# Attention steps two half chunks apart, projections in turns in the halves of one PSUM bank, DMA-made blocks in a value chunk's second half, first operands copied

## The chip, the cores and the metric

The kernel runs on one core of one Trainium2 chip. The metric is the device time of one execution in microseconds; a time is the median of several runs. The engines are named as in the profile: PE (TensorE, the matrix engine), DVE (VectorE), ACT (ScalarE), POOL (GpSimd) and SP (SyncE, which issues most transfers).

## The reference

A two-layer encoder on 256 tokens of width 2048, in fp32. Each layer is an attention part and an MLP of hidden width 8192:

```python
for i in range(DEPTH):                                   # 2 layers
    n = rms_norm(h, attn_norm[i])
    if i % N_MIXERS == 0:                                # layer 0: neighbourhood attention
        z = n @ a_w_in[j]
        q, k, v, qm = jnp.split(z, [MIX_WIDTH, 2 * MIX_WIDTH, 3 * MIX_WIDTH], axis=-1)
        mix = neighbourhood_attention(...)               # 12 heads of 128, a bias per head
    else:                                                # layer 1: grouped-query attention
        ...
    km, vm = jnp.split(m @ w_mem_kv[i], 2, axis=-1)
    cross = memory_attention(...)                        # 4 heads, 256 memory tokens
    h = h + jnp.concatenate([mix, cross], axis=-1) @ w_o[i]
    n = rms_norm(h, mlp_norm[i])
    h = h + jnp.square(jax.nn.relu(n @ w_up[i])) @ w_down[i]
return rms_norm(h, final_norm)
```

The change lies in layer 0's attention part: the projections to `qm` (4 memory heads), `q` and `k` (12 mix heads each) and `v` (12 heads), and the heads' scores, softmax and product with the values.

## The kernel before

**Exact products.** Every fp32 operand x is split in two: `hi`, a copy in the matrix engine's format made by ACT (L500), and `lo` = x - hi, made by DVE (L501). A product is three matmuls: hi·hi, lo·hi and hi·lo.

**Chunks.** Weights are read in chunks of 128x2048 fp32 (1024 KB). A chunk is worked in two half chunks, and the half chunk is the clock of the program. `run_all` goes through a list of half chunks; `ahead` runs the stages of later ones: their load eight half chunks ahead, their `pre` five and their `prep` (the splits) three. `later(n, fn)` runs `fn` n half chunks later. What comes out is handed to a scheduler that simulates the engines and may still move instructions; its result is the order that the listings below show.

**Projections (kind S).** One chunk makes one head's q, k or qm, transposed: 48 matmuls of 128x256 into a PSUM tile `ps_s` (L404). DVE reads it out scaled by the norm's row factor (`summed`, L545: qm_s, q_s, k_s); ACT and DVE split the result (qmT, qT, kT). There are 4 + 12 x 2 = 28 such chunks. With a chunk that follows one of another kind, `entered_half` makes the first 128 columns of lo apart from the rest.

**Values.** The values of a group of four heads come from four chunks by a scheme of seven products instead of eight: p1 to p7, each summed over the chunks in half a bank of PSUM (`v_ps`, four banks; tile ps_v, L882). `value_grains` (L838 to L890) gives each value chunk two half chunks ("grains"). Of a chunk's four 512-column blocks b0 to b3, products p1, p2 and p4 use a block as it was loaded or with another added, the others use sums of blocks. `pre` makes these in `v_t`: one copy on ACT (L849), two sums on DVE (L850, L852), and two on DMA, which adds while it moves: POOL issues b3 += b1 in the loaded tile (raw<-raw) and block 2 of v_t += block 1 (v_t<-v_t). The left operands are parts of the normed input, or its sums (`left`, made by `x_d` on DVE, L823, and a split). After the fourth chunk `values_done` combines the seven products (v_c, L903) and splits the result into `va` (L693 on ACT, L694 on DVE).

**Heads.** `attention` runs each head in four steps at set distances in half chunks: `attend` (scores into `sc_ps`, L557 to L559, bias L566, max L568, exp L570, 1/sum L573, scale L578); `turned` (DVE transposes in 32x32 squares, L615, and four SP transfers that put the squares in place, L620, tile pT_t); `halved` (pT_t is split); `attend3` (av, L634 to L636, then the split into `cat`). The distances are in `steps`, counted from `at`: (0, 1, 3, 4), starting one half chunk after the projection.

**Order around the change.** The plan alternates: one projection chunk, then one value half chunk (two of them behind the fifth and sixth projection), until the 24 value half chunks are used up; the last projections follow each other.

**Room.** In layer 0, PSUM has five banks in the pool `acc` and three in `att` (scores and av). `v_ps` holds four of acc's banks while a value group is summed, so that one is left for projections. The pools: ring (tiles `raw`, three; hi and lo, four), `spare` (`sums`: one v_t), work, `cat`, which also has a small unused tile `pad`.

Of the kernel before, what the change touches and what calls it, by code (L numbers as in the profile page):

```python
# [10 lines left out]
F32 = mybir.dt.float32  # L11
F32R = mybir.dt.float32r
BF16 = mybir.dt.bfloat16
AF = mybir.ActivationFunctionType
ALU = mybir.AluOpType
AX = mybir.AxisListType

P = 128
D = 2048
SEQ = 256  # L20
# [4 lines left out]
NH = 12  # L25
NKV = 4
NMH = 4
# [7 lines left out]
HALF = CH // 2  # L35
# [26 lines left out]
LEFT = 16  # L62
# [95 lines left out]

class Grain:

    kind, last_block = "G", False

    def __init__(self, run, after=None, load=None, pre=None, prep=None, ahead=(8, 5, 3)):
        self.run, self.after, self.stages, self.ahead = run, after, (load, pre, prep), ahead
# [3 lines left out]
def encoder_kernel(ctx: ExitStack, tc: tile.TileContext, t: dict, out: bass.AP):  # L168
    nc = tc.nc
# [27 lines left out]
    def open_ring():  # L197
        at.ring = opened("ring")
        at.cat = opened("cat")

        for pool in (at.ring, at.cat):
            pool.tile([P, 64], F32, tag="pad", name="pad")

    def open_work():
        at.work = opened("work", side="right", bufs=2)
# [25 lines left out]
    for q in range(4):  # L231
        s = slice(q * 512, (q + 1) * 512)
# [113 lines left out]
    def new_half(kind):  # L346
        s = slice(STILL_AT // 4, STILL_AT // 4 + HALF) if kind == "S" else slice(0, HALF)
        return tuple(at.ring.tile([P, HALF + n], F32R, tag=x, bufs=4, name=x)[:, s] for x, n in LONGER.items())
# [11 lines left out]
    def later(n, fn, *args):  # L360
        pending.append((state["tick"] + n, fn, args))
# [105 lines left out]
    def add_s(src, acts, done, place=None):  # L467

        def start(w):
            if place != 1:  # L470
                box["ps_s"] = at.acc.tile([P, 512], F32, tag="acc", name="ps_s")
            w.ps = box["ps_s"][:, (place or 0) * SEQ :][:, :SEQ]
        plan.append(Work("S", src, acts, 0, True, True, start, done))
# [24 lines left out]
    def split(dst_hi, dst_lo, src):  # L498

        first = nc.scalar.activation(dst_hi, src, AF.Copy)  # L500
        return first, nc.vector.tensor_tensor(dst_lo, src, dst_hi.bitcast(F32), op=ALU.subtract)  # L501
# [141 lines left out]
    def attention(jobs, at, gap=1, steps=(0, 1, 3, 4), rest=0):  # L643


        def step(n, job, prev):
            qT, kT, bias, v, head, cat = job
            if n == 0:
                res = attend(qT, kT, bias)
            elif n == 1 and len(steps) == 4:  # L650
                res = turned(prev)
            elif n < len(steps) - 1:
                res, box["pT", head] = (halved if len(steps) == 4 else attend2)(prev)
            else:
                if "between" not in box:
                    return attend3(prev, v, head, cat)
                with tc.issue_after(box.pop("between").ins):
                    return attend3(prev, v, head, cat)
            results[n, head] = res

        results = {}
        for t in range(len(jobs) + len(steps) - 1):
            for n in range(len(steps)):
                if 0 <= t - n < len(jobs):
                    j = t - n
                    more = rest if n == len(steps) - 1 and j == len(jobs) - 1 else 0
                    later(at + gap * j + steps[n] + more,
                          lambda n=n, job=jobs[j]: step(n, job, results.get((n - 1, job[4]))))
# [4 lines left out]
    def get(name):  # L673
        return lambda: box[name]
# [8 lines left out]
    def keys(name):  # L683
        return at.work.tile([P, NMH, 512], F32R, tag="keys", bufs=1, name=name)
# [4 lines left out]
    def head_of(v, hd):  # L689
        return lambda part, kt: (box[v] if isinstance(v, tuple) else v)[:, part, kt, hd * HD : (hd + 1) * HD]  # L690
# [59 lines left out]
            add_s(t[f"w_km{layer}"][hd], get("memT"), km_done(layer, hd), 1 if (layer, hd) == (0, 3) else None)  # L750
        add_m([t[f"w_vm{layer}"][c] for c in range(4)], parts_of("memT"), vm_done(layer), layer == 0)

    mem_sq = at.work.tile([P, 512], F32, tag="b_o", bufs=3, name="mem_sq")

    def mem_squares(j):
        m = mem0[:, j * 512 : (j + 1) * 512]
# [73 lines left out]

    GH = 4

    PARTS = (("p3", "p1", "p2", "p5"), ("p7", "p6", "p4"))
    PLACES = {"p3": (0, 0), "p1": (0, 1), "p2": (1, 0), "p5": (1, 1), "p7": (2, 0), "p6": (2, 1), "p4": (3, 0)}
    RAW = {"p1": (0, 1), "p2": (1, 1), "p4": (1, 0)}
    SUM = {"p5": 0, "p7": 1, "p6": 2, "p3": 3}

    def value_grains(g, c, begins, ends):  # L838

        own = {}  # L840

        def load():
            own["b"] = at.ring.tile([P, CH], F32, tag="raw", bufs=3, name="raw")
            nc.sync.dma_start(own["b"], t["w_av"][g * 4 + c])

        def pre():
            b = own["b"].rearrange("p (a b) -> p a b", a=4)
            s = own["t"] = at.spare.tile([P, 3, 512], F32, tag="sums", name="v_t")
            nc.scalar.activation(s[:, 2, :], b[:, 2, :], AF.Copy)  # L849
            nc.vector.tensor_tensor(s[:, 0, :], b[:, 3, :], b[:, 0, :], op=ALU.add)  # L850
            nc.gpsimd.dma_start(b[:, 3, :], b[:, 1, :], accum_op=ALU.add)
            nc.vector.tensor_tensor(s[:, 1, :], s[:, 0, :], b[:, 1, :], op=ALU.add)  # L852
            nc.gpsimd.dma_start(s[:, 2, :], s[:, 1, :], accum_op=ALU.add)

        def prep(n):
            src = own["t"].rearrange("p a b -> p (a b)") if n else own["b"]
            for m in range(2):
                x = src[:, m * HALF : min((m + 1) * HALF, src.shape[-1])]
                hi, lo = (y[:, : x.shape[-1]] for y in new_half("S"))
                split(hi, lo, x)  # L860
                own[n, m] = hi, lo

        def left(name, q, part):
            if name in RAW:
                e, i = RAW[name]
                return box["nT"][:, (2 * c + q) * 2 + e, part * SEQ + i * P :][:, :P]
            return box["left", c][:, q, part, SUM[name], :]

        def run(n):
            if begins and n == 0:  # L870
                box["v_ps"] = [at.acc.tile([P, 512], F32, tag="acc", name="ps_v") for _ in range(4)]
            for m in range(2):
                hi, lo = own.pop((n, m))
                for q in range(2):
                    for a, name in enumerate(PARTS[n][2 * m : 2 * m + 2]):
                        bank, half = PLACES[name]
                        ps = box["v_ps"][bank][:, half * SEQ : (half + 1) * SEQ]
                        s = slice(a * 512 + q * SEQ, a * 512 + (q + 1) * SEQ)
                        begin, end = begins and q == 0, ends and q == 1
                        for part, x, st, sp in ((0, hi, begin and half == 0, False), (0, lo, False, False),  # L880
                                                (1, hi, False, end)):
                            ins = nc.tensor.matmul(ps, left(name, q, part), x[:, s], start=st, stop=sp,  # L882
                                                   skip_group_check=True)
                            if x is hi and part == 0:
                                pin(ins)

        def after():
            if ends:
                values_done(g)

        return [Grain(lambda: run(0), None, load, pre, lambda: prep(0)),
                Grain(lambda: run(1), after, None, None, lambda: prep(1))]

    def values_done(g):

        p = {name: box["v_ps"][bank][:, half * SEQ : (half + 1) * SEQ] for name, (bank, half) in PLACES.items()}
        c = at.work.tile([P, NT, 2, SEQ], F32, tag="pT", name="v_c")
# [19 lines left out]
    def a_k_done(hd):  # L917
        def f(w):
            k = at.work.tile([P, 512], F32R, tag="b_y2", name="kT")
            s = summed(w.ps, "k", box["x_row"])  # L920
            split(k[:, :SEQ], k[:, SEQ:], s)
            b = at.work.tile([P, BJ * GRID_W], F32, tag="b_o", bufs=3, name="bias")
            nc.sync.dma_start(b, t["bias"][hd])
            attention([(box.pop(("q", hd)), k, b, head_of(("v", hd // GH), hd % GH), hd, box["cat"])], 1)
        return f

    def a_qm_done(hd):
        def f(w):
            if hd == 0:
                box["cat"] = at.cat.tile([P, KT, 512], F32R, tag="cat", name="cat0")  # L930
            q = at.work.tile([P, 512], F32R, tag="b_y", name="qmT")
            s = summed(w.ps, "qm", box["x_row"], SCALE)
            split(q[:, :SEQ], q[:, SEQ:], s)
            attention([(q, box["km"][:, hd, :], None, head_of(box["vm"], hd), NH + hd, box["cat"])], 1)
        return f

    CHUNKS = (2, 0, 1, 3)
    with_values = [x for g in range(NH // GH) for n, c in enumerate(CHUNKS) for x in value_grains(g, c, n == 0, n == 3)]
# [1 line left out]
    for hd in range(NH):  # L940
        projections += [(t["w_aq"][hd], a_q_done(hd)), (t["w_ak"][hd], a_k_done(hd))]
    for n, (src, done) in enumerate(projections):
        add_s(src, get("nT"), done)
        for _ in range(1 + (n in (4, 5))):
            if with_values:
                plan.append(with_values.pop(0))
# [833 lines left out]
```

## Time and profile before

| | us |
|---|---|
| median of 3 runs | 2050.93 (2050.22 to 2051.31) |
| profiled execution, its own time | 2049.45 |
| its span | 2047.6 |
| attention part of layer 0 in which PE is not full | about 101 to 380 |

The page gives each engine's busy time, then the span in 40 equal slices of 51.2 us with the busy share in tenths; `PEclk` is the clock granted to PE. The windows view cuts the span at chosen times. The waits view sums what an engine's instructions waited for. A row of a timeline gives start, duration, engine, line, operation, and in brackets the idle time before it with what ended it.

### The profile page before, as it was taken

How to read it: one execution, taken by the hardware profiler on the slowest of the kernel's cores; microseconds unless marked ns; L12 is line 12 of the kernel's file. 1: busy time of each engine (PE TensorE's matmuls, PEld its weight loads, DVE VectorE, ACT ScalarE, POOL GpSimd, SP SyncE). 2: the span in 40 equal slices, each digit the busy share in tenths (PEclk: the TensorE clock that was granted, in tenths of full speed). 3: DMA queues.
4: the chain of work that ended last, by engine and by line, in shares of the span. 5: the costliest groups of instructions: out<-in, count | busy, mean ns of one | idle time of the engine just before them, and what ended most of it. 6: DMA issues, size and time to landing. Idle time of an engine off the chain costs nothing.

```text
span 2047.6 us, 33383 instructions
## 1 busy us (share of the span) xinstructions
PE 2006.2 (98%) x13136; PEld 1826.6 (89%) x13136; DVE 1760.5 (86%) x2126; ACT 1376.8 (67%) x1933; POOL 144.3 (7%) x169
## 2 busy tenths in 40 slices
PE   9977989999999999999999999999999999999998
PEld 8877989989999999999998888889999999999997
DVE  7777788668989999999999778778989999999997
ACT  6755656557777777777776566566777777777774
POOL 0001010000000000000000011000000000000000
PEclk9988999999999999999999999999999999999999
DMA  7856677667777777777765865368777777777772
GB/s 298 290 171 170 206 205 256 205 221 235 230 236 232 226 237 231 227 237 229 236 225 167 290 193 196 129 229 264 232 224 240 226 238 232 221 243 227 228 235 103
DMA packets 109311, 456.46 MB, mean 223 GB/s; under 512 B 11360, under 2 KB 38752, under 8 KB 61536
## 3 DMA queue, kind: packets, MB, share of 16 engines
q1 hardware_dynamic: 88704, 417.08, 58.0%
q0 software_dynamic: 20160, 36.71, 11.0%
q8 instruction: 103, 1.69, 0.3%
q10 hardware_dynamic: 288, 0.52, 0.1%
q14 instruction: 56, 0.46, 0.1%
HBM read 400.27 MB, written 4.19 MB: 198 GB/s over the span
## 4 chain that ended last, share of the span: by engine, by line
PE 92%; DVE 3%; DMA 2%; issue 1%; ACT 1%; SPq 0%; DVEq 0%; POOL 0%; POOLq 0%; ACTq 0%
PE ps_u L404 34%; PE p L1230 9%; PE p L1228 9%; PE p L1231 9%; PE ps_s L404 7%; PE ps_m L381 6%; PE ps_m L385 6%; PE ps_m L384 6%; PE ps_v L882 2%; DVE lo L501 1%; DMA mem_k<-km_w 1%; DMA raw<-in_w_aqm 1%; ACT hi L500 0%; PE av L635 0%; PE av L636 0%
## 5 line engine op out<-in xcount | busy, mean ns | idle before, releaser
L404 PE MATMUL ps_u<-hT,uh 128*128 128x256 f32 x3812 | 663.4, 276 | 0.0
L404 PEld LDWEIGHTS ps_u<-hT,uh 128*128 128x128 f32 x3812 | 578.9, 188 | 5.5
L404 PE MATMUL ps_u<-hT,ul 128*128 128x256 f32 x1960 | 541.4, 276 | 0.0
L500 ACT ACTIVATE uh<-raw_U 128x1024 fp32r<-128x1024 f32 x262 | 277.2, 1060 | 208.4 <-PE ps_u L404 195.6
L404 PEld LDWEIGHTS ps_u<-hT,ul 128*128 128x128 f32 x1960 | 368.0, 188 | 0.0
L501 DVE TENSOR_TENSOR lo<-raw,hi 128x1024 fp32r<-128x1024 f32 (+1 forms) x218 | 258.3, 1192 | 97.7 <-ACT hi L500 96.8
L501 DVE TENSOR_TENSOR ul<-raw_U,uh 128x1024 fp32r<-128x1024 f32 x262 | 319.1, 1222 | 15.5 <-ACT uh L500 15.5
L501 DVE TENSOR_TENSOR tl<-t,th 128x2048 fp32r<-128x2048 f32 x116 | 265.8, 2291 | 71.4 <-ACT th L500 71.0
L500 ACT ACTIVATE hi<-raw 128x1024 fp32r<-128x1024 f32 (+1 forms) x218 | 223.3, 1035 | 150.8 <-PE ps_m L385 74.2
L500 ACT ACTIVATE th<-t 128x2048 fp32r<-128x2048 f32 x116 | 222.9, 1921 | 118.1 <-PE p L1231 114.8
L501 DVE TENSOR_TENSOR bl<-b,bh 128x1536 fp32r<-128x1536 f32 x116 | 203.3, 1753 | 0.0
L1228 PE MATMUL p<-th,a_s 128*128 128x512 f32 x464 | 181.2, 391 | 0.0
L1197 POOL DMA_DIRECT2D t<-b x116 | 100.3, 865 | 1144.4 <-ACT t L1196 1052.6
L1230 PE MATMUL p<-tl,a_s 128*128 128x512 f32 x464 | 181.0, 390 | 0.0
L1231 PE MATMUL p<-th,a_s 128*128 128x512 f32 x464 | 180.5, 389 | 0.0
L500 ACT ACTIVATE bh<-b 128x1536 fp32r<-128x1536 f32 x116 | 172.8, 1490 | 7.7
L404 PE MATMUL ps_s<-nT,hi 128*128 128x256 f32 x896 | 159.9, 279 | 7.5 <-DVE k_s L545 4.6
L404 PEld LDWEIGHTS ps_s<-nT,hi 128*128 128x128 f32 x896 | 136.6, 188 | 9.0 <-ACT hi L500 5.0
L1231 PE MATMUL p<-bh,a_s 128*128 128x512 f32 x348 | 136.2, 391 | 0.0
L1230 PE MATMUL p<-bl,a_s 128*128 128x512 f32 x348 | 135.7, 390 | 0.0
L1228 PE MATMUL p<-bh,a_s 128*128 128x512 f32 x348 | 135.4, 389 | 0.0
L404 PE MATMUL ps_s<-nT,lo 128*128 128x256 f32 x448 | 124.9, 279 | 2.1 <-DVE lo L501 2.1
(328 smaller groups left out, 3788.7 us busy)
## 6 DMA issues: line engine op xcount, KB each, us to landing
raw_U<-in_w_up SPq DMA_DIRECT2D x128, 1024.0 KB, 5.5
b<-in_w_pair SPq DMA_DIRECT2D x116, 1024.0 KB, 5.8
raw<-in_w_o SPq DMA_DIRECT2D x32, 1024.0 KB, 5.0
t<-b POOLq DMA_DIRECT2D x116, 256.0 KB, 5.2
raw<-in_w_b SPq DMA_DIRECT2D x21, 1024.0 KB, 5.1
raw<-in_w_av SPq DMA_DIRECT2D x12, 1024.0 KB, 5.0
raw<-in_w_aq SPq DMA_DIRECT2D x12, 1024.0 KB, 5.4
raw<-in_w_ak SPq DMA_DIRECT2D x12, 1024.0 KB, 5.1
```

The source lines that it names most:

```text
L381: first = nc.tensor.matmul(ps, ah, hi[:, s], start=st, stop=False)
L384: nc.tensor.matmul(ps, ah, lo[:, s], start=False, stop=False)
L385: final = nc.tensor.matmul(ps, al, hi[:, s], start=False, stop=sp)
L404: ins = nc.tensor.matmul(ps, x, acts[:, k, part], start=k == n == 0, stop=k == KT - 1 and n == 2)
L500: first = nc.scalar.activation(dst_hi, src, AF.Copy)
L501: return first, nc.vector.tensor_tensor(dst_lo, src, dst_hi.bitcast(F32), op=ALU.subtract)
L882: ins = nc.tensor.matmul(ps, left(name, q, part), x[:, s], start=st, stop=sp, skip_group_check=True)
L1197: nc.gpsimd.dma_start(s[:, 3, :], b[:, 1, :], accum_op=ALU.add)
L1228: ins = nc.tensor.matmul(ps, a[:, 0, ai, :], hi[:, s], start=begins, stop=False)
L1230: nc.tensor.matmul(ps, a[:, 0, ai, :], lo[:, s], start=False, stop=False)
L1231: nc.tensor.matmul(ps, a[:, 1, ai, :], hi[:, s], start=False, stop=ends)
```

## The change

Six edits, all for layer 0's attention part.

1. A projection that follows a value half chunk now counts as following another kind (`Grain.kind` "M"), so its lo is made in two pieces (128 and 896 columns) and the first matmuls go lo before hi.
2. All 28 projections share one tile `ps_s` of acc, and take its left and right 256 columns in turns.
3. Products p5 and p7 change places: both blocks that DMA finishes (for p4 and p5) are now used in a value chunk's second half. v_t has four blocks instead of three; ACT copies two; the first DMA adds into v_t instead of the loaded tile. `prep` splits five pieces instead of four.
4. The memory heads and mix heads 0 to 7 start two half chunks after their projection and take their steps at (0, 2, 4, 6); heads 8 to 11 keep one and (0, 1, 3, 4).
5. Eight 128x128 left operands, those of the first matmul of each value half chunk, are copied by ACT to a place of their own (`entries`), eight half chunks after the last memory head; from then on those matmuls read the copies.
6. `cat`'s unused tile is gone, and a tile `mem_sq` used at the very start moves from the work pool to `spare`.

```diff
 class Grain:
-    kind, last_block = "G", False
+    kind, last_block = "M", False
...
-        for pool in (at.ring, at.cat):
-            pool.tile([P, 64], F32, tag="pad", name="pad")
+        at.ring.tile([P, 64], F32, tag="pad", name="pad")
...
     def add_s(src, acts, done, place=None):
         def start(w):
+            if place == "turns":
+                if "turns" not in box:
+                    box["turns"] = [0, at.acc.tile([P, 512], F32, tag="acc", name="ps_s")]
+                box["turns"][0] += 1
+                w.ps = box["turns"][1][:, box["turns"][0] % 2 * SEQ :][:, :SEQ]
+                return
             if place != 1:
                 box["ps_s"] = at.acc.tile([P, 512], F32, tag="acc", name="ps_s")
...
-    mem_sq = at.work.tile([P, 512], F32, tag="b_o", bufs=3, name="mem_sq")
+    mem_sq = at.spare.tile([P, 512], F32, tag="sums", name="mem_sq")
...
-    PARTS = (("p3", "p1", "p2", "p5"), ("p7", "p6", "p4"))
-    PLACES = {"p3": (0, 0), "p1": (0, 1), "p2": (1, 0), "p5": (1, 1), "p7": (2, 0), "p6": (2, 1), "p4": (3, 0)}
+    PARTS = (("p3", "p1", "p2", "p7"), ("p6", "p4", "p5"))
+    PLACES = {"p3": (0, 0), "p1": (0, 1), "p2": (1, 0), "p7": (1, 1), "p6": (2, 0), "p4": (2, 1), "p5": (3, 0)}
...
         def pre():
-            s = own["t"] = at.spare.tile([P, 3, 512], F32, tag="sums", name="v_t")
-            nc.scalar.activation(s[:, 2, :], b[:, 2, :], AF.Copy)
+            s = own["t"] = at.spare.tile([P, 4, 512], F32, tag="sums", name="v_t")
+            nc.scalar.activation(s[:, 2:4, :], b[:, 2:4, :], AF.Copy)
             nc.vector.tensor_tensor(s[:, 0, :], b[:, 3, :], b[:, 0, :], op=ALU.add)
-            nc.gpsimd.dma_start(b[:, 3, :], b[:, 1, :], accum_op=ALU.add)
+            nc.gpsimd.dma_start(s[:, 3, :], b[:, 1, :], accum_op=ALU.add)
...
         def prep(n):
-            src = own["t"].rearrange("p a b -> p (a b)") if n else own["b"]
-            for m in range(2):
-                x = src[:, m * HALF : min((m + 1) * HALF, src.shape[-1])]
-                hi, lo = (y[:, : x.shape[-1]] for y in new_half("S"))
-                split(hi, lo, x)
-                own[n, m] = hi, lo
+            b, s = own["b"], own["t"].rearrange("p a b -> p (a b)")
+            for m, src in enumerate(((s[:, 512 : 1536], s[:, 1536:]) if n else (b[:, :HALF], b[:, HALF : 1536], s[:, :512]))):
+                if m < 2:
+                    own[n, m] = new_half("S")
+                at_ = slice(0, src.shape[-1]) if m < 2 else slice(512, HALF)
+                split(*(x[:, at_] for x in own[n, min(m, 1)]), src)
...
-                            ins = nc.tensor.matmul(ps, left(name, q, part), x[:, s], start=st, stop=sp,
-                                                   skip_group_check=True)
+                            entry = "entry" in box and m == q == a == part == 0 and x is hi
+                            ah = box["entry"][:, n, c, :] if entry else left(name, q, part)
+                            ins = nc.tensor.matmul(ps, ah, x[:, s], start=st, stop=sp, skip_group_check=True)
...
-            attention([(box.pop(("q", hd)), k, b, head_of(("v", hd // GH), hd % GH), hd, box["cat"])], 1)
+            attention([(box.pop(("q", hd)), k, b, head_of(("v", hd // GH), hd % GH), hd, box["cat"])],
+                      *((2, 1, (0, 2, 4, 6)) if hd < 8 else (1,)))
...
-            attention([(q, box["km"][:, hd, :], None, head_of(box["vm"], hd), NH + hd, box["cat"])], 1)
+            attention([(q, box["km"][:, hd, :], None, head_of(box["vm"], hd), NH + hd, box["cat"])], 2, 1,
+                      (0, 2, 4, 6))
+            if hd == NMH - 1:
+                later(8, copied)
...
+    def copied():
+        room = keys("entries").rearrange("p a b -> p (a b)")[:, LEFT + 8 :][:, : 2 * 4 * P]
+        box["entry"] = room.rearrange("p (n c j) -> p n c j", n=2, c=4)
+        for n, name in enumerate(("p3", "p6")):
+            for c in range(4):
+                nc.scalar.activation(box["entry"][:, n, c, :], box["left", c][:, 0, 0, SUM[name], :].bitcast(F32), AF.Copy)
...
-        add_s(src, get("nT"), done)
+        add_s(src, get("nT"), done, "turns")
```

What the built programs have in place of this, at three places. First PE, around the first memory head's scores (ps_s is the projection, sc_ps the scores, ps_v a value product). Before:

```order
L404 MATMUL ps_s_1129<-nT0_926,hi_1093 128x256 x2
L404 MATMUL ps_s_1129<-nT0_926,lo_1094 128x256
L557 MATMUL sc_ps_1203<-km_568,qmT_1198 128x256
L558 MATMUL sc_ps_1203<-km_568,qmT_1198 128x256
L559 MATMUL sc_ps_1203<-km_568,qmT_1198 128x256
...
L882 MATMUL ps_v_1224<-hi_1121,left_1028 128x256
L882 MATMUL ps_v_1224<-lo_1122,left_1028 128x256
```

With the change:

```order
L403 MATMUL ps_s_1130<-nT0_925,hi_1092 128x256 x2
L403 MATMUL ps_s_1130<-nT0_925,lo_1093 128x256
L889 MATMUL ps_v_1209<-hi_1120,left_1027 128x256
L889 MATMUL ps_v_1209<-lo_1121,left_1027 128x256
...
L403 MATMUL ps_s_1130<-nT0_925,hi_1170 128x256 x2
L403 MATMUL ps_s_1130<-nT0_925,lo_1171 128x256
L562 MATMUL sc_ps_1237<-km_567,qmT_1200 128x256
L563 MATMUL sc_ps_1237<-km_567,qmT_1200 128x256
```

The scores stood directly behind their projection; now a whole value half chunk (24 matmuls) and 21 matmuls of the next projection stand between.

Second DVE, from the first splits of the memory heads' stretch to the first sum (qm_s, the read of the first projection). Before:

```order
L501 TENSOR_TENSOR lo_1126<-raw_953,hi_1125 128x1024
L501 TENSOR_TENSOR lo_1170<-raw_1167,hi_1169 128x1024
L823 TENSOR_TENSOR x_d_1158<-xT_851 128x2x128 x2
L545 SCALAR_TENSOR_TENSOR qm_s_1199<-ps_s_1129,x_row_999 128x256
L823 TENSOR_TENSOR x_d_1158<-x_d_1158,xT_851 128x2x128
L501 TENSOR_TENSOR lo_1221<-raw_1167,hi_1220 128x1024
```

With the change:

```order
L506 TENSOR_TENSOR lo_1125<-raw_952,hi_1124 128x512
L506 TENSOR_TENSOR lo_1125<-v_t_1055,hi_1124 128x512
L828 TENSOR_TENSOR x_d_1159<-xT_850 128x2x128 x2
L354 TENSOR_TENSOR lo_1171<-raw_1168,hi_1170 128x128
L354 TENSOR_TENSOR lo_1171<-raw_1168,hi_1170 128x896
L828 TENSOR_TENSOR x_d_1159<-x_d_1159,xT_850 128x2x128
L828 TENSOR_TENSOR x_d_1286<-xT_848 128x2x128 x2
L550 SCALAR_TENSOR_TENSOR qm_s_1201<-ps_s_1130,x_row_998 128x256
```

The sum qm_s was the fourth of these rows and is now the eighth; lo_1171 (lo_1170 before) comes in two pieces.

Third PE, where one of the last projections follows the one before it, with the engines that each row waits for. Before, in two tiles, with no wait at the second one's start:

```order
L404 MATMUL ps_s_4110<-nT0_926,hi_4071 128x256 x2
L404 MATMUL ps_s_4110<-nT0_926,lo_4072 128x256
L404 MATMUL ps_s_4205<-nT0_926,hi_4106 128x256 x2
L404 MATMUL ps_s_4205<-nT0_926,lo_4107 128x256
L404 MATMUL ps_s_4205<-nT0_926,hi_4137 128x256 [waits Activation_49]
```

With the change, in one tile:

```order
L403 MATMUL ps_s_1130<-nT0_925,hi_4010 128x256 x2
L403 MATMUL ps_s_1130<-nT0_925,lo_4011 128x256
L403 MATMUL ps_s_1130<-nT0_925,hi_4065 128x256 [waits DVE_49]
L403 MATMUL ps_s_1130<-nT0_925,hi_4065 128x256
L403 MATMUL ps_s_1130<-nT0_925,lo_4066 128x256
```

The first matmul of a projection now waits for DVE, which reads the sum of the projection before it out of the same bank.

## The prediction

> **What bounds the kernel now.** I read the busy times and the 40 slices of the page first, to see which engine fills the span and where it does not.
>
> ```profile
> PE 2006.2 (98%) x13136; PEld 1826.6 (89%) x13136; DVE 1760.5 (86%) x2126; ACT 1376.8 (67%) x1933; POOL 144.3 (7%) x169
> PE   9977989999999999999999999999999999999998
> PEclk9988999999999999999999999999999999999999
> ```
>
> TensorE (PE) is the bound almost everywhere; a slice is 51.2 us, and only slices 3 to 5 (102 to 256 us) show PE below nine tenths, slices 3 and 4 also a lower granted clock. That is the attention half of layer 0, the place of the change. I cut it at four times with the windows view (columns: length, then busy time and instructions of PE, PE's loads, DVE, ACT, POOL, then the granted clock, DMA share and GB/s) and add the stretches before and behind it.
>
> ```profile
> 0.00:101.60 101.60, 100.09 (x652) 90.85 (x652) 76.56 (x119) 72.92 (x124) 3.77 (x10) 1.00 0.80 293
> 101.60:179.50 77.90, 62.07 (x466) 59.82 (x465) 54.95 (x83) 43.75 (x77) 6.93 (x8) 0.91 0.62 177
> 179.50:223.50 44.00, 36.94 (x279) 35.58 (x277) 31.75 (x47) 22.44 (x34) 3.45 (x4) 0.88 0.61 180
> 223.50:339.50 116.00, 107.90 (x894) 106.45 (x895) 91.83 (x132) 69.39 (x116) 8.63 (x10) 0.99 0.73 225
> 339.50:379.30 39.80, 39.79 (x343) 39.80 (x344) 32.89 (x52) 24.94 (x45) 0.00 (x0) 1.00 0.64 213
> 379.30:2047.60 1668.30, 1659.45 (x10512) 1494.10 (x10510) 1472.52 (x1694) 1143.38 (x1541) 121.51 (x137) 1.00 0.69 222
> ```
>
> Call the four middle stretches A (memory heads and the first value group), B, C (two thirds of the mix heads) and D (the last ones). PE idles 15.83 us in A, 7.06 in B, 8.10 in C and 0.01 in D: 31.0 in all. Its clock was lower in A and B; where PE worked without gaps it was 1.00. The lost clock is worth at most (1 - 0.91) x 77.9 = 7.0 in A, 0.12 x 44.0 = 5.3 in B and 0.01 x 116 = 1.2 in C, 13.5 us. So 44.5 us is all that better order can give here; everything behind 379.30 keeps its instructions and is left at zero.
>
> What PE waits for between 101 and 380 us (total, times, longest):
>
> ```profile
> PE sc_ps L557 <- ACT qmT L500: 6.5, 2, 4.3
> PE ps_s L404 <- DVE k_s L545: 4.6, 6, 1.5
> PE av L634 <- ACT pT_t L500: 3.9, 2, 3.4
> PE av L634 <- ACT va L693: 3.3, 1, 3.3
> PE sc_ps L557 <- ACT kT L500: 3.2, 2, 1.9
> PE ps_s L404 <- DVE qm_s L545: 3.0, 2, 1.8
> PE av L635 <- DVE pT_t L501: 2.1, 3, 0.9
> PE ps_s L404 <- DVE lo L501: 2.1, 1, 2.1
> ```
>
> Two kinds. Scores and av wait for the step before them of the same head (qmT, kT, pT_t, va: 19.0 of these 28.7 us); projections wait for the previous sum to leave the single free bank of acc (k_s, qm_s: 7.6 us). The change touches both.
>
> **The change, part by part.**
>
> *Steps two half chunks apart.* The longest wait, in PE's and ACT's timelines and the chain of waits:
>
> ```profile
> 101.57 0.28 PE L404 MATMUL ps_s<-nT,lo 128*128 128x256 f32 x1
> 106.17 0.58 PE L557 MATMUL sc_ps<-km,qmT 128*128 128x256 f32 x1 [4.33 <-ACT qmT L500]
> 107.86 0.58 PE L559 MATMUL sc_ps<-km,qmT 128*128 128x256 f32 x1 [0.90 <-DVE qmT L501]
> 105.25 0.42 DVE L545 SCALAR_TENSOR_TENSOR qm_s<-ps_s,x_row 128x256 f32<-128x256 f32 x1
> 102.34 2.00 ACT L500 ACTIVATE hi<-raw 128x1024 fp32r<-128x1024 f32 x2 [4.01 <-DMA raw<-in_w_aqm]
> 96.84 5.40 DMA raw<-in_w_aqm
> 293.54 2.82 PE ps_v L882 x24
> 288.09 5.45 PE ps_s L404 x48
> ```
>
> The projection ends at 101.85; its sum is read only at 105.25, behind split work for a load that landed at 102.24, and scores start at 106.17. The idle time is 4.33 + 0.90 = 5.2 us. In the new order a value half chunk (24 matmuls, 2.82 us) and 21 projection matmuls (21/48 of 5.45 = 2.4) stand between: 5.2 us of work, just enough. The same holds for the wait on kT (3.2 us) and for pT_t: each later step gains at least a half chunk. The wait for va is one of three at the end of the first value group:
>
> ```profile
> 178.00 1.65 PE ps_v L882 x14
> 179.64 5.46 PE ps_s L404 x48
> 188.41 0.58 PE L634 MATMUL av<-pT_t,va 128*128 128x256 f32 x1 [3.32 <-ACT va L693]
> 190.47 0.58 PE L636 MATMUL av<-pT_t,va 128*128 128x256 f32 x1 [0.42 <-DVE va L694]
> ```
>
> From the group's end (179.64) to va's lo part (190.4) it takes 10.8 us. Until now 5.46 us of projection stood between, plus scores; afterwards the order has about 13.7 us of PE work there, by counting its matmuls at these prices. So this wait should vanish too. What the moved step issues goes with it: the four pT transfers stand on SP one weight load later than before. They hold SP for 2.5 us, and a weight load queued behind them starts that much later:
>
> ```profile
> 256.47 2.53 SPq L620 DMA_DIRECT2D pT_t<-sc_t  x4
> 262.31 0.33 SPq L289 DMA_DIRECT2D raw<-in_w_ak  x1
> raw<-in_w_aqm SPq DMA_DIRECT2D x4, 1024.0 KB, 6.3
> ```
>
> Loads are issued eight half chunks ahead (four 5.45 us chunks or more) for about 6 us of flight, so 2.5 us is covered; without that cover it is 2.5 us per head, up to 16 times. The DMA share is 0.62 in A against 0.80 in the first stretch, so the bandwidth for a shorter A (177 x 77.9/61 = 226 GB/s, against 293) is there.
>
> *What is late next.* When PE no longer idles, it meets the start of the next projection. That one must wait for the previous sum, which sits in DVE's queue behind lo pieces and x_d (the DVE rows above the prediction: qm_s comes eighth there, after two x_d groups; before it came fourth). Rows for DVE's pieces:
>
> ```profile
> L501 DVE TENSOR_TENSOR lo<-raw,hi 128x1024 fp32r<-128x1024 f32 x66 | 80.1, 1222 | 33.0 <-ACT hi L500 33.0
> 104.58 0.75 DVE L823 TENSOR_TENSOR x_d<-xT 128x256 f32<-128x256 f32 x2
> ```
>
> One or two lo pieces (1.2 us each) or x_d (0.75) ahead of it give 0.6 to 2 us per start. Walking A by these prices, I get about 2.0, 1.4, 1.4, 0.6 and 1.4 at the five starts: 6.8 us, of which a little is covered; I take 6. DVE itself is 54.95 us busy in A, so A can't shrink below about 55, a gain of at most 22.9. A: 15.83 + 7.0 - 6 = **-17** (bounds: -22.8, and 0 if the same waits come back at other places). B: 7.06 + 5.3 - 4 = **-8** (-12.3 to 0). C: 8.10 + 1.2 - 3 = **-6.3** (-9.3 to 0); there are six heads in C, and half a microsecond left over per head is my choice, near the shortest wait on k_s below.
>
> *Turns in one bank.* Nothing is freed by it alone: the built order makes each projection's first matmul wait for DVE's sum of the one before. While value half chunks stand between, their 2.1 to 2.8 us cover most of it. Behind the last value chunk (D) nothing stands between four of five starts, the fifth has o-projection matmuls before it, and where there were several free banks and 0.01 us idle, there is now a wait each:
>
> ```profile
> 339.51 0.47 PE L404 MATMUL ps_s<-nT,hi 128*128 128x256 f32 x2 [0.61 <-DVE k_s L545]
> ```
>
> The least is 0.61 us (this row, with DVE free), the most 1.5 (the longest of the six above). DVE is 83% busy in D, so I take 1.0. D: 4 x 1.0 = **+4** (2.4 to 6.0). The Trainium skill ("PSUM — Partial Sum Buffer", section "PSUM bank collisions raise a hardware error") says that two engines may not touch one bank and quadrant at once even in disjoint columns, and that waits go by bank, not by address. By that rule the halves can't overlap, which agrees with the waits of the built order; no run so far shows a start in one half during a sum in the other. If halves were independent, D would cost nothing, and the sum would be 4 us lower.
>
> *DMA-made blocks later, five splits instead of four, `entry` copies, M instead of G.* DVE gets 34 more instructions (a 128-column piece of lo for 22 chunks, one more v_t piece for each of 12 value chunks). The nearest row is rs (160 ns) below and a 512-wide piece above:
>
> ```profile
> L501 DVE TENSOR_TENSOR lo<-v_t,hi 128x512 fp32r<-128x512 f32 x12 | 8.2, 682 | 0.8 <-ACT hi L500 0.8
> L573 DVE RECIPROCAL rs<-sm 128x2 f32<-128x2 f32 x12 | 1.9, 160 | 3.3 <-ACT sc L570 3.3
> L500 ACT ACTIVATE cat<-av 128x256 fp32r<-128x256 f32 x11 | 4.2, 382 | 14.9 <-PE av L636 14.9
> ```
>
> The column counts split are the same, so only the fixed part is new: 0.16 to 0.3 each (0.3: two pieces of 682 ns against one of 1222 leave 0.14, and a wait between), 5 to 10 us over 278, hidden while DVE has its 21% free in C. Eight copies on ACT cost under 8 x 0.38 = 3 us on an engine 51 to 60% busy: nothing. If DVE had no room, the 5 to 10 us would come on top. The earlier blocks take a wait off splits that the trace doesn't show PE to have (no DMA releases a value matmul in the waits above): nothing. One small gain: chunks run at two cadences.
>
> ```profile
> 333.23 5.69 PE ps_s L404 x48
> ```
>
> Against 5.45 for the same 48 that is 0.24. What sets the cadence no row tells; another first operand and another order of hi and lo may. For 20 slow chunks it is 4.8 at most; with nothing for or against, I take **-2** (0 to -4.8).
>
> **Sum.** -17 - 8 - 6.3 + 4 - 2 = -29.3. The profiled execution took 2049.45 us (span 2047.6), so 2020.1; the median of the three runs is 2050.93, 1.5 above it. Forecast: **2021.5 us**, 1.4% faster.
>
> **Rivals.**
>
> *DVE is the new bound in A* (chance 0.20). Its queue in A would be 54.95 plus the new pieces in 61 us, over 90%. If PE waits at each start for a full lo piece and more, half the gain is given back: A -8, B -5, C -5, D +5, cadence -1: -14, or **2037**. For it: 33.0 us of DVE idling in front of lo pieces waits for ACT, so it isn't free at will. Against: it is 70% busy in A now, and the value half chunks cover it.
>
> *All of it* (0.10). New waits of 1 to 2 us per stretch: A -20, B -10, C -8, D 0, cadence -4: -42, or **2009**. The residual waits above speak against it.
>
> *The change doesn't do what it says* (0.05). The scheduler's order moves the steps but each projection now waits as long as its scores did: **2050**. Against: the order does show work between.
>
> *Slower: one bank for all projections* (0.08). Each of 27 starts behind another projection waits for a sum in DVE's queue. What can be won is 44.5 + 2 = 46.5 us, so it decides from 46.5/27 = 1.72 us per start. Two lo pieces (2 x 1.22) ahead of the sum, less a covered part, make 2.3: 27 x 2.3 = 62, +15.6, or **2066**. For it: 1.8 us waits on qm_s and 1.5 on k_s exist already. Against: most starts now have a value half chunk in front, longer than this wait.
>
> **Chances and range.** The forecast has 0.57. About 4 us (0.2%) is what the runs can tell from no change. Faster: 0.57 + 0.20 + 0.10 = 0.87; within: 0.05; slower: 0.08. The range goes from **2006** (the upper gain, with cadence at its bound) to **2038** (DVE as the bound), leaving out the slower case, no change, and half of the large gain, 0.18.
>
> **What would show it.** PE's waits on qmT, kT and va gone from A to C, and the granted clock there at 0.97 or more. PE's remaining waits all on qm_s, q_s or k_s, 0.6 to 2 us each. D with some 4 us idle where it had none. A near 61 us, B near 36, C near 110. Wrong would be: PE still idle on pT_t or on raw loads, clock still at 0.9, or waits on q_s of over 2 us each.

## The result: 14 us faster, less than half of the forecast

The changed kernel takes 2036.73 us (median of 4 runs, 2032.87 to 2038.10) against 2050.57 before (4 runs): 0.993 of the time, 95% interval 0.9913 to 0.9947. That is -13.8 us; the forecast was -29.

The page of the changed kernel (busy times, PE's slices and the granted clock):

```profile
PE 2000.8 (99%) x13136; PEld 1820.6 (90%) x13136; DVE 1759.0 (87%) x2160; ACT 1381.6 (68%) x1953; POOL 142.4 (7%) x169
PE   9999997999999999999999999999999999999998
PEclk9999999999999999999999999999999999999999
```

Slices 3 and 4, the weak ones before, are full; slice 7 (305 to 355 us), which was full, is now the weak one. The stretches A to D of the prediction, cut at the same work (the starts of projections 7, 11 and 23, and the last projection's end), in the windows view of the changed kernel:

```profile
101.60:165.50 63.90, 59.30 (x475) 58.48 (x474) 54.30 (x92) 45.19 (x83) 6.95 (x8) 0.95 0.71 215
165.50:199.50 34.00, 33.85 (x291) 33.43 (x290) 30.27 (x53) 24.08 (x41) 3.44 (x4) 1.00 0.74 231
199.50:311.20 111.70, 105.76 (x885) 103.15 (x883) 91.19 (x151) 72.17 (x122) 8.60 (x10) 1.00 0.76 240
311.20:364.40 53.20, 44.98 (x354) 43.70 (x355) 36.40 (x57) 26.34 (x47) 0.00 (x0) 0.94 0.49 161
```

A went from 77.9 to 63.9 us (-14.0), B from 44.0 to 34.0 (-10.0), C from 116.0 to 111.7 (-4.3): -28.3 together. D went from 39.8 to 53.2. Some 2.8 us of that are 12 matmuls of the output projection that now stand before the last projection; the other 10.6 are lost. PE idled 0.01 us in D and idles 8.2 now, at a clock of 0.94. Counted in another way: the last value matmul starts at 317.9 us instead of 348.5, 30.6 us earlier; from there to the first matmul of the MLP it takes 134.1 us instead of 120.9, 13.2 more. Some 21 more matmuls (2.4 us at 114 ns) now stand behind that mark, so for like work it is about 28.2 won and 10.8 lost, as in the stretches.

What PE waits for between 95 and 380 us, and its longest waits one by one (timeline):

```profile
PE av L639 <- ACT pT_t L505: 6.9, 4, 5.6
PE ps_s L403 <- DVE k_s L550: 4.3, 4, 3.0
PE ps_s L403 <- DVE lo L354: 3.0, 4, 2.0
PE ps_s L403 <- DVE qm_s L550: 2.1, 1, 2.1
PE ps_s L403 <- DVE q_s L550: 2.1, 2, 1.5
...
311.20 0.39 PE L403 MATMUL ps_s<-nT,lo 128*128 128x256 f32 x1 [3.03 <-DVE k_s L550]
322.19 0.50 PE L403 MATMUL ps_s<-nT,hi 128*128 128x256 f32 x2 [1.54 <-DVE q_s L550]
333.48 0.58 PE L639 MATMUL av<-pT_t,va 128*128 128x256 f32 x1 [5.56 <-ACT pT_t L505]
342.85 0.51 PE L403 MATMUL ps_s<-nT,hi 128*128 128x256 f32 x2 [0.52 <-DVE q_s L550]
349.18 0.48 PE L403 MATMUL ps_s<-nT,hi 128*128 128x256 f32 x2 [0.61 <-DVE k_s L550]
```

The waits on qmT, kT and va, 15.2 us with their smaller parts, are gone. New is 5.56 us at 333.48: av of head 8, the first head with the short distance, stands at the head of PE's queue and its transposed scores are not there. The chain of waits tells what came late (start, duration), and the windows view the clock behind it:

```profile
324.27 1.08 DVE sc_t L620 x2
325.40 0.55 SPq L625
...
327.94 4.76 DMA pT_t<-sc_t
332.80 0.64 ACT pT_t L505
333.48 0.58 PE av L639
334.06 4.13 PE ps_s L403 x23
...
333.40:337.10 3.70, 3.62 (x17) 3.62 (x18) 2.25 (x3) 1.28 (x3) 0.00 (x0) 0.50 0.13 22
```

The transposes are done at 325.3, four transfers take until 332.7, and the 23 projection matmuls behind av, which need none of this, run only then, at 180 ns each on average instead of 114: the granted clock was 0.50 from 333.4 to 337.1, which costs another 1.8 us. D's loss is thus 8.2 us of idle time (5.56 on pT_t, 2.7 at three starts of projections) and most of the rest the clock.

### The profile page after: what moved, and what is told of

It is laid out like the page before. It is cut to its first block, busy times and chain, and to the rows that moved or that the text cites. A ratio compares the mean times of both kernels' runs of the same rounds, so it can differ in the third digit from the quotient of the medians.

```text
span 2031.1 us, 33392 instructions
## 1 busy us (share of the span) xinstructions
PE 2000.8 (99%) x13136; PEld 1820.6 (90%) x13136; DVE 1759.0 (87%) x2160; ACT 1381.6 (68%) x1953; POOL 142.4 (7%) x169
## 4 chain that ended last, share of the span: by engine, by line
PE 90%; DVE 4%; DMA 3%; ACT 1%; issue 1%; SPq 0%; DVEq 0%; POOLq 0%; POOL 0%; ACTq 0%
PE ps_u L403 34%; PE p L1246 9%; PE p L1248 9%; PE p L1249 9%; PE ps_m L380 6%; PE ps_m L383 6%; PE ps_m L384 6%; PE ps_s L403 6%; DVE lo L506 1%; PE ps_v L889 1%; DMA raw<-in_w_ak 1%; DVE lo L354 1%; DMA pT_t<-sc_t 1%; SPq L625 0%; DMA raw<-in_w_aqm 0%
## 5 line engine op out<-in xcount | busy, mean ns | idle before, releaser
L506 DVE TENSOR_TENSOR lo<-raw,hi 128x1024 fp32r<-128x1024 f32 (+1 forms) x196 | 224.3, 1153 | 73.5 <-ACT hi L505 72.6
L505 ACT ACTIVATE hi<-raw 128x1024 fp32r<-128x1024 f32 (+1 forms) x196 | 194.7, 1004 | 104.7 <-PE ps_m L384 71.3
```

## Experiments

Two explanations of the lost 13 us were set against each other. **T**: the long distance makes the whole gain, and the return to the short distance at head 8 gives half of it back. **R**: the shared bank gives it back. Undoing one part at a time came first.

**Own tiles.**

```diff
-        add_s(src, get("nT"), done, "turns")
+        add_s(src, get("nT"), done)
```

> Only the shared bank is undone: each projection takes a new tile again. Theory T (the last heads' short distance gives the gain back: up to the last value matmul the changed kernel is 30.6 us ahead, and it loses 14 us between 300 and 343 us): the stretch up to the last value matmul stays as it is, because only one bank is free there anyway; at the end only the waits on k_s and q_s of 0.5 to 1.5 us go, so 1 to 4 us less than the changed kernel (2033 to 2036). Rival R (the shared bank gives the gain back): all waits of projections on sums go, 8.5 us, with the clock they cost 10 or more: 2027 or less.

Measured 2021.71 us (2020.33 to 2022.75), 0.9869 of before (0.9852 to 0.9885): 15.0 us better than the changed kernel. The time lies in R's range and not in T's. The only wait in its waits view from 300 to 365 us, and the window that answers D with its end:

```profile
309.33 0.40 PE L403 MATMUL ps_s<-nT,lo 128*128 128x256 f32 x1 [3.04 <-DVE k_s L550]
...
309.30:350.10 40.80, 40.77 (x341) 40.77 (x342) 32.71 (x52) 23.19 (x40) 0.00 (x0) 0.96 0.60 205
```

Behind 309.3 PE doesn't idle at all. The last value matmul is at 317.5, as in the changed kernel (317.9). So in this order the shared bank costs nothing while value half chunks stand between, and all of it behind. The wait of 3.0 us on k_s isn't its doing: it stands here with own tiles just as at 311.20 in the changed kernel. And the wait for pT_t is gone too, which is no wait for a bank.

The order shows why. Between the av of head 7 and that of head 8 PE has 49 projection matmuls in the changed kernel, 109 with own tiles. These are the rows of the built programs from the end of head 7's av on, changed kernel first:

```
av x5, ps_s x49, av x1, ps_s x23, av x5, sc_ps x1, ps_s x8, sc_ps x5, ps_s x96
av x5, ps_s x109, av x1, sc_ps x6, ps_s x10, av x5, ps_s x117
```

Sixty matmuls at 114 ns are 6.8 us of work that av lets pass with own tiles and holds up with the shared bank.

**Steps as before.**

```diff
-                      *((2, 1, (0, 2, 4, 6)) if hd < 8 else (1,)))
+                      1)
...
-            attention([(q, ..., box["cat"])], 2, 1, (0, 2, 4, 6))
+            attention([(q, ..., box["cat"])], 1)
```

> Only the steps' distance is undone: all heads start one half chunk after their projection, steps at (0, 1, 3, 4). T: nearly all of the 30.6 us won up to the last value matmul comes from the distance, so at most 5 of them stay; the 14 us lost behind it are not lost either: 2045 to 2053. Rival (blocks, kind M and copies make the gain): more than 15 us of the lead stay, 2037 or less.

Measured 2047.27 us (10 runs, 2044.10 to 2048.12), 0.999 of before (0.9981 to 1.0). Its waits between 95 and 400 us:

```profile
PE ps_s L403 <- DVE qm_s L550: 9.6, 3, 5.0
PE ps_s L403 <- DVE k_s L550: 7.4, 8, 1.8
PE ps_s L403 <- DVE lo L354: 7.1, 4, 3.7
PE av L639 <- ACT pT_t L505: 2.5, 1, 2.5
```

All other parts together give 1 to 2 us (2048.80 for the kernel before beside these runs). The gain is the distance's. T's total came, not its condition: 7.0 us of the lead stay up to the last value matmul (341.5 instead of 348.5), where T allowed 5, and 3.3 are lost behind it, where PE waits 1.76 and 1.51 us for sums (349.00 and 363.09). Where scores had waited for qmT, the next projection now waits for qm_s at the same place: 9.6 us.

**Long distance for all mix heads.**

```diff
-                      *((2, 1, (0, 2, 4, 6)) if hd < 8 else (1,)))
+                      *((2, 1, (0, 2, 4, 6)) if hd < 12 else (1,)))
```

> All 12 mix heads keep the long distance, nothing else differs. T: the wait of 5.6 us on pT_t and part of 3.0 us on k_s go, and the low clock behind them (1.5 us): 6 to 10 us less than the changed kernel, 2027 to 2031, unless the last head's values come too late for the output projection, which would show as a new wait behind 364 us. R: the waits on sums stay, within 3 us of the changed kernel.

Measured 2026.11 us (2022.95 to 2029.11): 10.6 less than the changed kernel, a little more than T's range. Its waits between 300 and 365 us:

```profile
PE ps_s L403 <- DVE k_s L550: 2.4, 3, 1.0
PE av L639 <- ACT pT_t L505: 1.5, 1, 1.5
PE av L640 <- DVE pT_t L506: 0.4, 1, 0.4
```

The wait for pT_t is down from 5.8 to 1.9 us, the waits on sums are smaller but there. So this speaks for T as well; each of two edits takes away most of the loss.

**Value blocks as before.**

```diff
-    PARTS = (("p3", "p1", "p2", "p7"), ("p6", "p4", "p5"))
+    PARTS = (("p3", "p1", "p2", "p5"), ("p7", "p6", "p4"))
... (PLACES, pre and prep as in the kernel before, p7 instead of p6 among the copies)
```

> Only the blocks of the value chunk are undone (p5 in the first half, DMA adding into the loaded tile, four splits). T: the changed kernel within 3 us, since no DMA released a value matmul before. Rival (the later blocks are what lets PE run without gaps): a wait of value matmuls on the summed blocks appears and 5 us or more are lost, 2042 or more.

Measured 2021.62 us (2019.70 to 2024.46): 15.1 better than the changed kernel, which neither side had expected. Here 75 projection matmuls stand between the two avs, with the bank still shared, and PE waits only for sums (its waits from 300 to 365 us; 0.82 of the 2.6 on k_s lies ahead of the last value matmul):

```profile
PE ps_s L403 <- DVE k_s L550: 2.6, 3, 1.2
PE ps_s L403 <- DVE q_s L550: 1.7, 2, 1.2
```

Three edits, of which two don't touch the heads' steps, each took 10 to 15 us off. Common to them is the order: av of head 8 comes later. This became the third theory: the loss is in PE's order, which the scheduler fixes from its own simulation, and the bank costs only its 4 us of waits besides.

**Only the last step later, bank shared.** This moves av alone.

```diff
-                      *((2, 1, (0, 2, 4, 6)) if hd < 8 else (1,)))
+                      *((2, 1, (0, 2, 4, 6)) if hd < 8 else (1, 1, (0, 1, 3, 6))))
```

> The changed kernel, bank still shared, but the last step of heads 8 to 11 two half chunks later (steps (0, 1, 3, 6)). The order now has 74 projection matmuls instead of 49 between the av of head 7 and the first matmul of head 8's av. If what is lost behind the last value matmul is mostly that av standing in PE's queue before its pT_t is there (5.6 us and 1.9 of low clock) and only 2.7 us are the bank's own: 2027 to 2031. If the bank's waits are the loss: 2034 or more.

Measured 2030.30 us (2028.93 to 2034.72). The number is in the range of the order theory: 6.4 us less than the changed kernel. But the profiled execution, the slowest of the four, shows the rest not to be 2.7 us of waits for sums (timeline, 318 to 352 us):

```profile
325.62 0.50 PE L403 MATMUL ps_s<-nT,hi 128*128 128x256 f32 x2 [1.30 <-DVE q_s L550]
332.50 0.47 PE L403 MATMUL ps_s<-nT,hi 128*128 128x256 f32 x2 [1.16 <-DVE k_s L550]
338.04 0.38 PE L562 MATMUL sc_ps<-kT,qT 128*128 128x256 f32 x1 [2.44 <-ACT kT L505]
344.47 0.50 PE L403 MATMUL ps_s<-nT,hi 128*128 128x256 f32 x2 [0.52 <-DVE q_s L550]
350.80 0.48 PE L403 MATMUL ps_s<-nT,hi 128*128 128x256 f32 x2 [0.61 <-DVE k_s L550]
```

The four starts behind the last value matmul cost 3.6 us, and scores of a later head now stand too early: 2.44 us. So moving av cures one such place and leaves about 8.6 us against own tiles (2030.30 - 2021.71), the bank's waits and the new one on kT together.

The second series puts single parts on top of the distance alone.

**The distance alone**, in the kernel before.

```diff
-            attention([(box.pop(("q", hd)), ..., box["cat"])], 1)
+            attention([(box.pop(("q", hd)), ..., box["cat"])], *((2, 1, (0, 2, 4, 6)) if hd < 8 else (1,)))
...
-            attention([(q, ..., box["cat"])], 1)
+            attention([(q, ..., box["cat"])], 2, 1, (0, 2, 4, 6))
```

> The kernel before with only the steps' distance changed (memory heads and mix heads 0 to 7 at 2 and (0, 2, 4, 6)). If the distance makes the whole gain and the shared bank gives half of it back: 2018 to 2024, like the changed kernel with its own tiles (2021.7) and about 28 us below the kernel before. If the distance needs the later blocks, the early piece of lo or the copies to show: a few us to 12 us worse than that, 2026 to 2034.

Measured 2017.53 us (2016.34 to 2019.06), 0.9843 of before (0.9829 to 0.9858): -32.2 us against the 2049.74 measured beside it, at the lower edge of what was expected, and 19 us below the whole change. All that PE still waits for between 95 and 400 us:

```profile
PE ps_s L404 <- DVE qm_s L545: 2.9, 1, 2.9
PE ps_s L404 <- DVE rs L573: 1.9, 2, 1.6
PE ps_s L404 <- ACT hi L500: 1.0, 1, 1.0
PE ps_s L404 <- DVE lo L501: 0.9, 1, 0.9
PE av L634 <- ACT pT_t L500: 0.6, 1, 0.6
PE av L635 <- DVE pT_t L501: 0.3, 1, 0.3
PE sc_ps L557 <- ACT qmT L500: 0.2, 1, 0.2
```

7.8 us in all, where it was 31.0, and with the short distance for heads 8 to 11. T falls as it stood: the return to the short distance costs nothing in this order.

**Distance and shared bank.** The edit is the change's `add_s` on top of the last kernel.

> Steps' distance and shared bank, nothing else of the change. If the bank costs its own waits at the four starts behind the last value matmul (0.7 to 1.4 us each, as with the blocks as before): 4 to 6 us over steps_alone (2017.5), 2021 to 2024. If it costs 15 us in any order: 2030 to 2034.

Measured 2025.47 us (2024.40 to 2027.96), 7.9 over the distance alone, between the two expectations; the last value matmul comes 1.8 us later than there (314.1 and 312.3). Behind 316 us (timeline):

```profile
318.51 0.47 PE L404 MATMUL ps_s<-nT,hi 128*128 128x256 f32 x2 [1.75 <-DVE q_s L551]
326.58 0.58 PE L640 MATMUL av<-pT_t,va 128*128 128x256 f32 x1 [2.38 <-ACT pT_t L506]
337.50 0.50 PE L404 MATMUL ps_s<-nT,hi 128*128 128x256 f32 x2 [0.52 <-DVE q_s L551]
344.06 0.47 PE L404 MATMUL ps_s<-nT,hi 128*128 128x256 f32 x2 [0.61 <-DVE k_s L551]
```

Again waits for sums and, with them, an av before its pT_t.

**Distance and blocks.** The changed kernel with own tiles, kind G and no copies.

> Steps' distance and the new blocks, without the shared bank, the early piece of lo and the copies. If the blocks cost by themselves (two more splits' fixed part per chunk on DVE and a wider copy on ACT): 4 to 6 us over steps_alone, 2021 to 2024. If they cost only together with the early piece of lo (the wait of 3.0 us on k_s behind that piece): 2016 to 2019.

Measured 2021.06 us (2019.62 to 2023.67), 3.5 over the distance alone, at the lower edge of the first expectation. The last value matmul comes at 315.1 us instead of 312.3; behind it nothing is lost. The two rows of its waits that grew most over the distance alone:

```profile
PE ps_s L403 <- DVE lo L506: 3.0, 3, 1.3
PE ps_s L403 <- DVE rs L578: 3.0, 2, 2.1
```

The start of the projection that waited 3.0 us for k_s in the changed kernel and with own tiles waits 0.61 us here (308.10). With kind M and the blocks as before it waits 0.82 (next experiment, 307.12; the same 0.82 in both runs with old blocks). So the 3.0 us come with the new blocks and kind M together, shared bank or not.

**Distance and kind M.**

```diff
-    kind, last_block = "G", False
+    kind, last_block = "M", False
```

> Steps' distance and kind M, nothing else. If the early piece of lo gives what I put down for cadence: 2 us less than steps_alone, 2015 to 2016. If it costs its two instructions on DVE: 2018 to 2020. With the copies it was 2016.2.

Measured 2016.69 us (2015.63 to 2018.60), 0.8 under the distance alone; the two intervals (0.9828 to 0.9855 and 0.9829 to 0.9858) don't tell them apart.

**Own tiles without copies.** The call of `copied` is left out.

> Own tiles as before, and without the copies of first operands; the matmuls keep their order. If the copies cost and give nothing: within 2 us of own_tiles (2021.7). If they quicken the cadence: up to 4.8 us more.

Measured 2022.01 us (2019.76 to 2023.43) against 2021.71: the copies do nothing that shows.

**Own tiles and blocks as before.**

> Own tiles and the value chunk's blocks as before. If both of the earlier runs were 15 us faster for the same reason (head 8's av comes later in PE's order, here after 106 projection matmuls instead of 49): nothing adds up, 2018 to 2023. If each had taken away a cost of its own, they add: 2007 to 2012.

Measured 2016.19 us (2015.41 to 2018.64), 0.9838 of before (0.9824 to 0.9853). It lies 2 us under the first expectation and 4 over the second. The two gains of 15 us were one gain, plus 5.5 us for the blocks by themselves (2021.71 - 2016.19); with blocks as before the shared bank costs 5.4 (2021.62 - 2016.19).

**Distance for all 12 heads, nothing else.**

```diff
-                      *((2, 1, (0, 2, 4, 6)) if hd < 8 else (1,)))
+                      *((2, 1, (0, 2, 4, 6)) if hd < 12 else (1,)))
```

> Steps' distance for all 12 mix heads, nothing else of the change. If the 10 us that the longer distance gave the last heads in the changed kernel came from the shared bank's order alone: within 3 us of steps_alone, 2015 to 2020. If the last heads gain by distance in themselves: 2008 to 2012.

Measured 2016.32 us (2015.55 to 2019.15): the same as with eight. The last heads gain by distance only where the bank is shared.

**Two more profiles of the changed kernel.**

> The changed kernel once more, unchanged, for another profile: its four executions spread from 2032.9 to 2038.1 and the profile at hand is of the fastest. If the spread lies where head 8's av waits for pT_t (5.6 us in the first profile, the transfer landing 4.8 us after its last issue): that wait differs between the profiles by about as much as the spans do, and the time up to the last value matmul (317.9) stays within 1 us. If it lies elsewhere, the wait stays at 5 to 6 us.

> The same kernel a third time, with the same two readings: the wait for pT_t and the time of the last value matmul.

Measured 2034.78 and 2035.30 us. The same row in both:

```profile
333.90 0.58 PE L639 MATMUL av<-pT_t,va 128*128 128x256 f32 x1 [4.96 <-ACT pT_t L505]
```

```profile
335.84 0.58 PE L639 MATMUL av<-pT_t,va 128*128 128x256 f32 x1 [5.40 <-ACT pT_t L505]
```

The wait is there each time, 5.0 to 5.6 us, and the last value matmul comes at 319.0 and 320.4 instead of 317.9, 1.1 and 2.5 us later where the spans are 1.9 and 2.4 longer (2033.0 and 2033.5 against 2031.1). So the loss is a steady one and most of the spread lies ahead of it; what spreads there was not followed up.

Together, with the two marks of the profiled executions (us). The rows before and all but the distance have 666 matmuls in the trace from the one mark to the other, the others 684 to 690, so some 2 us of the last column are moved work:

| kernel | median | last value matmul | from there to the MLP |
|---|---|---|---|
| before | 2050.57 | 348.5 | 120.9 |
| the change | 2036.73 | 317.9 | 134.1 |
| all but the distance | 2047.27 | 341.5 | 124.2 |
| distance alone | 2017.53 | 312.3 | 123.0 |
| distance, bank | 2025.47 | 314.1 | 132.7 |
| distance, blocks | 2021.06 | 315.1 | 122.2 |
| change with own tiles | 2021.71 | 317.5 | 122.7 |
| change with old blocks | 2021.62 | 313.3 | 128.3 |
| change with own tiles, old blocks | 2016.19 | 313.7 | 123.0 |
| change, av later | 2030.30 | 321.6 | 132.3 |

The parts from 2050: distance -32, bank +8, blocks +3.5, kind M and copies nothing measurable; that makes 2029. The 7.7 us left to 2036.7 come with bank and blocks together; moving head 8's av alone took 6.4 us off. Such differences between runs are good to about 2 us: the kernel before, measured beside each series, came out at 2050.57, 2048.80, 2049.74 and 2049.03. Taken against these, distance, bank and blocks are -32.2, +8.7 and +4.2, and 5.5 is left; own tiles gain 13.3 instead of 15.0 (12.5 between the two profiled executions). That av stands in front of ready work is seen; that the scheduler puts it there because its simulation sees the projections held up by the bank is only argued. The distance alone, with or without M or the last heads, beats both kernels by far: 2016 to 2018 us.

## Why the prediction was wrong

**The waits it named, and what they were worth: right in the main.** A to C were to give -31.3 us and gave -28.3; the 30.6 to the last value matmul includes 2.4 of moved work. By stretch: A -17 forecast, -14.0 measured; B -8 and -10.0; C -6.3 and -4.3. C came out 2.0 short; the 3.0 us wait on k_s at its end, which comes with blocks and kind M together, is more than that. The distance alone gives -32.2. That waits on qmT, kT and va vanish was right; a granted clock of 0.97 or more came in B and C (1.00), not in A (0.95). One reading of the page was off without touching the sum: the slices below nine tenths before are 3, 4 and 6, not 3 to 5.

**The term that failed is D, +4.** It priced four starts of projections at 1.0 us and nothing else, on the reading that the shared bank costs what the row before shows for a wait on k_s. D lost 10.6 us. The starts were not what it got wrong: three of the four waited 1.54, 0.52 and 0.61 us, 2.7 together, and the other stands right behind head 8's av and shows no wait of its own. What failed is the step that takes PE's order in D as given by the plan and puts nothing on the avs. I had read that order at the starts of projections, not at the avs. In its place the runs showed head 8's av in front of ready work, waiting 5.56 us for pT_t, and 1.8 us of low clock behind it. Counting would have shown it: from head 8's last score matmul (315.8) the new order leaves 12.1 us to the end of the rows in front of its av (327.9), while the chain from there to the split pT_t took 17.6 us (14.8 with own tiles, where the order leaves 17.0). About 2.6 us of the 5.56 are slower transfers, whose cause stays open (last section); those no count of rows shows. "PE still idle on pT_t" stood there among the signs of an error, without a price.

**Blocks at nothing: wrong by 3.5 to 5.5 us.** The cover named was DVE's free fifth in C. The waits on lo, rs and k_s that grew say that it doesn't cover them where the splits fall; that the splits alone make the loss was not tested.

**Cadence, -2:** not to be seen; with kind M alone -0.8 within the noise.

**The bank rule.** The Trainium skill ("PSUM — Partial Sum Buffer", section "PSUM bank collisions raise a hardware error") says to guard PSUM with semaphores by bank and quadrant, or simply by bank, and not by address. The built program does so: behind the last value matmul, starts in the shared bank waited for the other half's sum, and with own tiles 40.8 us passed with no such wait. These waits are the program's own, so no run here shows what halves used at once would do. That independent halves would make "the sum 4 us lower" priced only those waits; own tiles, which change the order too, make it 13 to 15 lower.

**The rivals.** "DVE is the new bound in A" named 2037 us, which is what came, but by luck: it had A to C at -18, and they gave -28. So the measured time lies inside the range, at an end that was put there for another reason. The slower case needed 1.72 us at all 27 starts; the waits for sums come to 8.5 us in all.

## What to carry to other kernels

Where an order fixed beforehand puts an instruction that waits in front of ready ones, all that stands behind it waits too (here 5.56 us, and 1.8 more at the lower clock); so count, at each consumer, the work in front of it in the new order against the chain that feeds it. A resource that costs little where work covers it costs again where the cover ends, and moves other things there: look at the last heads apart from the others. And when an edit has six parts, time the one that carries the gain alone; here it gave 32 us and the whole 14.

## What the runs showed of the hardware that was not expected

Transfers of the same kind took longer in one order than in another, at about the same time of the program. Between 318 and 336 us, changed kernel and own tiles (median us from issue to landing):

```profile
raw<-in_w_ak SPq DMA_DIRECT2D x1, 1024.0 KB, 7.9
pT_t<-sc_t SPq DMA_DIRECT2D x4, 64.0 KB, 5.8
```

```profile
raw<-in_w_ak SPq DMA_DIRECT2D x1, 1024.0 KB, 4.9
pT_t<-sc_t SPq DMA_DIRECT2D x4, 64.0 KB, 3.2
```

The two more profiles of the changed kernel have 5.5 and 5.6 us for pT_t and the run with av later 5.7, so it isn't chance. With the bank shared and the blocks as before it was 2.8, with distance and bank alone 3.3. What held them up wasn't found; without it head 8's av would have waited some 2.6 us less (an estimate, the difference of the two medians). The 109 matmuls in front of it with own tiles would have covered all but about half a microsecond of the slower one.

The granted clock didn't follow the length of the gap before it. After 2.10 us of idle PE (to 107.93) the changed kernel had 0.50 from 109.5 to 111.8. After 3.03 us (to 311.20) it kept 1.00 up to 313.8, and with own tiles, after 3.04 us at the same place (to 309.33), the clock was 0.51 from 310.5 to 313.0.
